# Another PSUM ring for the transposed probabilities of the second attention layer

## The chip, the core and the metric

The kernel runs on one core of a Trainium2 chip. The metric is the device time of one execution in microseconds (us), as the median of several runs. Lower is better. The core has five engines that run side by side, each with its own queue: TensorE (PE in the profile, with its weight loads as PEld), VectorE (DVE), ScalarE (ACT), GpSimd (POOL) and SyncE (SP), which issues the DMAs. TensorE writes its results to PSUM, which has eight banks here of 128 x 512 fp32 values each.

## What is computed

Two decoder layers on one sequence of 256 positions and 1024 features, in fp32. Layer 0 is causal attention with 16 heads (with 256 positions there is one block, so the block-sparse form comes down to that). Layer 1 is a sliding-window attention of width 128 with a learned sink per head; its 16 query heads share four key and value heads. After each attention comes a gated feed-forward part with a causal convolution of width 3. The attention of layer 1, which is the part that matters here, cut down:

```python
def swa_sink_attention(q, k, v, sinks):
    ...
    logits = jnp.einsum('bkgnqd,bknpd->bkgnqp', qb, kcat).astype(jnp.float32) * (HEAD_DIM ** -0.5)
    rel = (jnp.arange(WINDOW)[:, None] + WINDOW) - jnp.arange(2 * WINDOW)[None, :]
    band = (rel >= 0) & (rel < WINDOW)
    ...
    logits = jnp.where(mask, logits, NEG)
    ...
    m = jnp.maximum(jnp.max(logits, axis=-1, keepdims=True), sink)
    e = jnp.exp(logits - m)
    p = e / (jnp.sum(e, axis=-1, keepdims=True) + jnp.exp(sink - m))
    out = jnp.einsum('bkgnqp,bknpd->bkgnqd', p.astype(v.dtype), vcat)
```

With 256 positions there are two blocks of 128 queries. The first block sees its own 128 keys, the second sees all 256 (the window cuts a triangle out of each half).

## The kernel before, in words

**Precision.** Each large product is made of three fp32r products: both operands are split into a high and a low part, and high x high, high x low and low x high are added up in PSUM. The weights come from memory as raw fp32 units of 128 x 2048, and ACT writes their high part (`hi_part`, L181), DVE their low part (`lo_part`, L186 and L188). These conversions run all the time, for the weights that are needed a few units later.

**PSUM.** `bank(tag)` (L94) gives out the eight banks in three rings: four banks of tag `acc`, two of `t`, two of `u`. A bank comes free when the last reader of its tile is done. A new tile takes whichever bank of its tag is free.

**Attention.** `attention` (L405) works on four groups g = 0 to 3 of four heads each, and a group on two pairs of heads, j = 2g and 2g + 1. It serves both layers; `sink=True` is layer 1. For one group of layer 1 the steps are:

1. `scores` (L420). The scores of the first query block, called diagonal here, are six matmuls (L429 to L431) with full 128 rows into one bank, `sd`. That bank is of tag `acc` while the output projection has not begun to accumulate (groups 0 and 1), and of tag `t` afterwards (groups 2 and 3). The scores of the second block against all 256 keys are the half-row scores: twelve matmuls (L436) that each use only 64 of the 128 rows of TensorE, one head of a pair in the lower half and one in the upper, into two banks of tag `u`: `sb` for one head of each pair and `sa` for the other.
2. `softmax` (L441), for each pair: masked minima on DVE (L454, one instruction for a head's diagonal scores, one for its half-row scores), the exponentials on ACT (L465), on POOL the sum of the two halves of the second block's row (L460; `merge`, which the window allows), and the division by the row sum on DVE and ACT (L470 to L477).
3. `merged_T` (L485), for each pair: four transposes on TensorE (L490) into one PSUM bank, a copy by ACT (L499) and a masked product by DVE (L496) to SBUF. In layer 0 `probs_T` does this in another way.
4. `values` (L524): sixteen matmuls (L535) of the transposed probabilities with the values, into one bank of tag `t` (two banks for the last group), then a high part by ACT (L542) and a low part by DVE (L543).

In program order the scores of group g + 1 stand between the transposes of group g and its values.

**Filler.** Between these steps `fill` puts other TensorE work: the second half of the query projection (L342 to L344), and then the first three of the four units of the output projection (`Down`, L566; matmuls L584 to L587). Unit i of the output projection needs the values of group i. The query projection hands over its result by `to_feature` (L379): four transposes (L383) into a bank of tag `t`, then copies by ACT (L394) and DVE (L389). Its second half does this once for each query block, while groups 0 and 1 are in work. The scores of groups 2 and 3 read what it delivers: the diagonal ones need the first block's, the half-row ones the second block's. After the attention the last unit of the output projection follows (`finish`), then the feed-forward part, whose matmuls are L677 to L679.

**Order.** The order up to the first scores of layer 0 is that of the code. After that (`manual.close()`, L548) a scheduler orders each engine's queue when the program is built: it goes through the program with durations of its own, and an engine takes the instruction that stands first in program order among those whose inputs are there and for whose tile a bank of the tag is free. So a later instruction can be queued ahead of an earlier one that is not yet ready. (In the last group of layer 1 ACT alone keeps the program's order, L560.)

Of the kernel before, what the change touches and what calls it, by code (L numbers as in the profile page):

```python
# [61 lines left out]
def trunk(ctx: ExitStack, tc, x, xw, pos, cpk, fin, w, out):  # L62
# [9 lines left out]
    def nm(s):  # L72
        uid[0] += 1
        return f"{s}_{uid[0]}"
# [5 lines left out]
    def spaced(pool, n, dt, tag, name, bufs):  # L80
        return pool.tile([P, n + ROUND], dt, tag=tag, name=name, bufs=bufs)[:, SKIP:SKIP + n]
# [12 lines left out]
    def bank(tag):  # L94
        return ps.tile([P, 512], F32, tag=tag, name=nm(tag), bufs=4 if tag == "acc" else 2)
# [35 lines left out]
    def tick(ns):  # L131
        clock[0] += ns
        while put_off and not busy[0]:
            item = min(put_off, key=lambda t: t[0])
            if item[0] > clock[0]:
                return
            run_item(item)

    def chain(key, *steps, urgent=0):

        def run(k):
            if urgent:
                with tc.high_priority(offset=urgent):
                    steps[k][1]()
            else:
                steps[k][1]()
            if k + 1 < len(steps):
                put_off.append((clock[0] + steps[k + 1][0], key, lambda: run(k + 1)))
        put_off.append((clock[0] + steps[0][0], key, lambda: run(0)))
# [85 lines left out]
    for c in range(KC):  # L235
        t, at = (first[c // 2], KC * (c == 1) + c % 2 * CH) if c < 6 else (first[c - 3], 0)
# [26 lines left out]
    for b in range(NB):  # L263
        t = one.tile([P, NH, HD], F32, name=f"v{b}")
# [140 lines left out]
    def attention(qk, ready, filler, lead, rate, msk, vcol, sink):  # L405
# [78 lines left out]

        def merged_T(j, pr):  # L485

            tp = bank("u").rearrange("p (e k t) -> p e k t", e=2, k=2)
            for e in range(2):
                for k in range(2):
                    nc.tensor.transpose(tp[:, e, k], pr[e][:, 2 * k * P:(2 * k + 1) * P], ident)  # L490
            tick(440)
            pT = spaced(qd, 4 * S, F32, "q", nm("pT"), 15)[:, :6 * P].rearrange("p (e k t) -> p e k t", e=2, k=3)

            def part():
                shape = [P, 2, 2, P]
                nc.vector.tensor_tensor(out=pT[:, :, 1:], in0=tp[:, :, 1:].to_broadcast(shape),  # L496
                                        in1=near.unsqueeze(1).to_broadcast(shape), op=ALU.mult)

            chain(("pT", j), (200.0, lambda: nc.scalar.activation(pT[:, :, 0], tp[:, :, 0], AF.Copy)), (100.0, part))  # L499
            return [pT[:, e].rearrange("p k t -> p (k t)") for e in range(2)]  # L500

        def probs_T(j, pr):
            require("sm", j)
            if sink:
                return merged_T(j, pr)
            out_ = []
            for e in range(2):
                tp = bank("u")
                for i in range(3):
                    nc.tensor.transpose(tp[:, i * P:(i + 1) * P], pr[e][:, i * P:(i + 1) * P], ident)  # L510
                tick(330)
                pT = row3()

                def copy(e=e, tp=tp, pT=pT):
                    if e:
                        nc.scalar.activation(pT, tp[:, :3 * P], AF.Copy)
                    else:
                        nc.vector.tensor_copy(pT, tp[:, :3 * P])

                chain(("pT", j), (200.0, copy))  # L520
                out_.append(pT)
            return out_
# [666 lines left out]
```

## Time and profile before

| | |
|---|---|
| median of 3 runs | 549.57 us (549.19 to 550.01) |
| the profiled execution, its own time | 549.75 us |
| its span, first to last instruction | 548.0 us |
| granted TensorE clock | 0.998 |
| TensorE matmuls busy | 540.5 us (99%), 3742 matmuls |
| TensorE weight loads busy | 496.7 us (91%) |
| DVE, ACT, POOL busy | 420.4 us (77%), 372.9 us (68%), 125.3 us (23%) |
| transposes L490 (layer 1) | 32 matmuls, into tag `u` |
| half-row scores L436 of layer 1 | 48 matmuls, 316.9 to 348.7 us |
| values L535 of layer 1 | 64 matmuls, 327.2 to 358.6 us |

The time of an execution is a little longer than the span, since it holds what lies before the first and after the last instruction. In the rows of a timeline the first number is the start in us from the span's beginning, the second the duration of the row; a row can hold several instructions of a kind (x12). Matmuls overlap in the array, so a row's duration is longer than the distance to the next row, and the distance is what the engine spent. An arrow `u<-q,q` says that a tile of tag `u` was written from two tiles named `q`. A bracket like `[0.46 <-PE u L436]` says that the engine stood idle for 0.46 us before this row, and what ended the wait.

### The profile page before, as it was taken

To read this page: it belongs to the slowest core of one execution; us is meant where nothing else is said; L and a number is where in the kernel's file an instruction comes from. 1 tells how busy PE (TensorE), PEld (TensorE's weight loads), DVE (VectorE), ACT (ScalarE), POOL (GpSimd) and SP (SyncE) were. 2 spreads that over 40 slices of the span, in tenths; PEclk is the share of its full clock that TensorE was granted. 3 is DMA by queue.
4 is the path that set the end of the run, shared out by engine and by line. 5 is a ranking of instruction groups with operands and counts; after the bars stand their busy time and mean duration, and the time that the engine had idled before them with its cause. 6 is when DMAs were issued, how large, how long until landed. Compare 5 with 4: busy or idle time off the path is not lost.

```text
span 548.0 us, 9909 instructions
## 1 busy us (share of the span) xinstructions
PE 540.5 (99%) x3742; PEld 496.7 (91%) x3742; DVE 420.4 (77%) x872; ACT 372.9 (68%) x731; POOL 125.3 (23%) x158
## 2 busy tenths in 40 slices
PE   9999999999999999999999999999999999999995
PEld 8888888899999999988888887879999999998884
DVE  6798778689899888864467789798898888884514
ACT  6989777677677777744348688787667777673314
POOL 8322102016223233120001024102332332310003
PEclk9999999999999999999999999999999999999999
DMA  8984444342655565565553534242375555666301
GB/s 317 392 269 172 172 154 175 135 154 78 215 210 202 220 231 209 188 229 220 197 188 154 181 127 155 77 154 83 150 249 213 203 193 221 250 225 222 112 0 77
DMA packets 16464, 100.99 MB, mean 184 GB/s; under 512 B 1952, under 2 KB 2080, under 8 KB 5920
## 3 DMA queue, kind: packets, MB, share of 16 engines
q1 hardware_dynamic: 16128, 100.09, 50.5%
q8 instruction: 29, 0.48, 0.4%
q10 hardware_dynamic: 288, 0.26, 0.1%
q14 instruction: 19, 0.16, 0.1%
HBM read 99.30 MB, written 1.05 MB: 183 GB/s over the span
## 4 chain that ended last, share of the span: by engine, by line
PE 93%; ACT 3%; DVE 3%; issue 0%; DVEq 0%; ACTq 0%
PE acc L584 9%; PE acc L585 9%; PE acc L587 9%; PE u L677 7%; PE u L679 7%; PE u L678 7%; PE t L679 6%; PE t L678 6%; PE t L677 6%; PE acc L342 5%; PE acc L343 5%; PE acc L344 5%; PE acc L789 2%; PE acc L679 2%; PE acc L678 2%; PE acc L677 2%
## 5 line engine op out<-in xcount | busy, mean ns | idle before, releaser
L186 DVE TENSOR_TENSOR wl<-wr,wh 128x1024 fp32r<-128x1024 f32 (+1 forms) x190 | 207.9, 1114 | 52.2 <-ACT wh L181 51.7
L181 ACT ACTIVATE wh<-wr 128x1024 fp32r<-128x1024 f32 (+1 forms) x190 | 176.5, 957 | 52.6 <-PE acc L587 42.8
L723 POOL TENSOR_TENSOR m<-m,m 128x256 f32<-128x256 f32 x44 | 70.4, 1601 | 166.5 <-DVE m L718 91.9
L584 PE MATMUL acc<-wh,q 128*128 128x512 f32 x238 | 92.4, 388 | 0.1
L585 PE MATMUL acc<-wl,q 128*128 128x512 f32 x238 | 90.8, 381 | 0.0
L677 PE MATMUL u<-q,wh 128*128 128x256 f32 x320 | 88.4, 277 | 0.0
L678 PE MATMUL u<-q,wh 128*128 128x256 f32 x320 | 88.2, 276 | 0.0
L679 PE MATMUL u<-q,wl 128*128 128x256 f32 x320 | 88.1, 276 | 0.0
L679 PE MATMUL t<-q,wl 128*128 128x256 f32 x288 | 79.3, 275 | 0.0
L677 PE MATMUL t<-q,wh 128*128 128x256 f32 x288 | 79.3, 275 | 0.0
L678 PE MATMUL t<-q,wh 128*128 128x256 f32 x288 | 79.3, 275 | 0.0
L587 PE MATMUL acc<-wh,q 128*128 128x512 f32 x238 | 75.4, 382 | 0.0
L678 PEld LDWEIGHTS u<-q,wh 128*128 128x128 f32 x320 | 61.5, 192 | 0.0
L679 PEld LDWEIGHTS u<-q,wl 128*128 128x128 f32 x320 | 61.5, 192 | 0.0
L677 PEld LDWEIGHTS u<-q,wh 128*128 128x128 f32 x320 | 61.3, 192 | 0.2 <-DVE q L305 0.2
L677 PEld LDWEIGHTS t<-q,wh 128*128 128x128 f32 x288 | 55.4, 192 | 0.0
L678 PEld LDWEIGHTS t<-q,wh 128*128 128x128 f32 x288 | 55.4, 192 | 0.0
L679 PEld LDWEIGHTS t<-q,wl 128*128 128x128 f32 x288 | 55.4, 192 | 0.0
L584 PEld LDWEIGHTS acc<-wh,q 128*128 128x128 f32 x238 | 45.1, 190 | 6.9 <-ACT q L542 0.9
L587 PEld LDWEIGHTS acc<-wh,q 128*128 128x128 f32 x238 | 44.9, 189 | 6.5 <-DVE q L543 0.3
L585 PEld LDWEIGHTS acc<-wl,q 128*128 128x128 f32 x238 | 45.2, 190 | 5.8 <-issue 0.3
L342 PE MATMUL acc<-wh,q 128*128 128x512 f32 x128 | 49.9, 390 | 0.0
(177 smaller groups left out, 1008.5 us busy)
## 6 DMA issues: line engine op xcount, KB each, us to landing
wr<-in_w SPq DMA_DIRECT2D x82, 1024.0 KB, 4.8
wr<-in_w SPq DMA_DIRECT2D x16, 512.0 KB, 6.4
first<-in_xw SPq DMA_DIRECT2D x7, 384.0 KB, 6.4
xr<-in_x SPq DMA_DIRECT2D x2, 512.0 KB, 8.0
fin_t<-in_fin SPq DMA_DIRECT2D x1, 512.0 KB, 5.5
out<-ot SPq DMA_DIRECT2D x1, 512.0 KB, 2.6
first<-in_xw SPq DMA_DIRECT2D x1, 388.0 KB, 3.5
out<-m ACTq DMA_DIRECT2D x1, 256.0 KB, 2.1
```

The costliest lines, as they stand in the source:

```text
L181: nc.scalar.activation(wq[i][0][:, c], raws[i][:, c], AF.Copy, **({} if g is None else {"scale": g}))
L186: nc.vector.tensor_tensor(out=lo, in0=raw, in1=hi, op=ALU.subtract)
L342: nc.tensor.matmul(o, xh[:, blk(b)], wh, start=(c == 0), stop=False)
L343: nc.tensor.matmul(o, xh[:, blk(b)], wl, start=False, stop=False)
L344: nc.tensor.matmul(o, xl[:, blk(b)], wh, start=False, stop=(c == KC - 1))
L584: nc.tensor.matmul(o, ph[:, blk(b)], turns(hi[:, s_]), start=first, stop=False)
L585: nc.tensor.matmul(o, ph[:, blk(b)], turns(lo[:, s_]), start=False, stop=False)
L587: nc.tensor.matmul(o, pl[:, blk(b)], turns(hi[:, s_]), start=False, stop=end)
L677: nc.tensor.matmul(o, hi[:, s_], xh, start=(c == 0), stop=False)
L678: nc.tensor.matmul(o, hi[:, s_], xl, start=False, stop=False)
L679: nc.tensor.matmul(o, lo[:, s_], xh, start=False, stop=(c == KC - 1))
L723: nc.gpsimd.tensor_tensor(out=h, in0=gs, in1=t[1], op=ALU.mult)
```

## The change

`merged_T` takes its bank from ring `t` and no longer from ring `u`. It is called only in layer 1, once for each of the eight pairs. Nothing else differs: the instructions, their sizes and the program order are the same.

```diff
         def merged_T(j, pr):
 
-            tp = bank("u").rearrange("p (e k t) -> p e k t", e=2, k=2)
+            tp = bank("t").rearrange("p (e k t) -> p e k t", e=2, k=2)
             for e in range(2):
                 for k in range(2):
                     nc.tensor.transpose(tp[:, e, k], pr[e][:, 2 * k * P:(2 * k + 1) * P], ident)
```

After it, ring `u` serves in this stage only `sa` and `sb` (two tiles for each group), and ring `t` serves the transposed probabilities (two tiles for each group), the values (one, in the last group two), the diagonal scores of groups 2 and 3, and the two `to_feature` tiles of the second half of the query projection.

## The prediction

> **What bounds the kernel now.** I read the page first.
>
> ```profile
> span 548.0 us, 9909 instructions
> ...
> PE 540.5 (99%) x3742; PEld 496.7 (91%) x3742; DVE 420.4 (77%) x872; ACT 372.9 (68%) x731; POOL 125.3 (23%) x158
> ...
> PE 93%; ACT 3%; DVE 3%; issue 0%; DVEq 0%; ACTq 0%
> ```
>
> TensorE is busy nearly everywhere, and 93% of the chain that ended last is TensorE work. So what TensorE no longer spends, or no longer waits for, in the attention of layer 1 comes off the end, since the feed-forward part behind it is its own back-to-back work. The table by stretches, from the values of one group to those of the next (groups 0 to 3), shows how full the others are there:
>
> ```profile
> 327.20:338.60 11.40, 11.19 (x74) 8.45 (x73) 10.88 (x40) 9.29 (x28) 4.76 (x8) 1.00 0.38 134
> 338.60:348.70 10.10, 10.10 (x66) 8.05 (x65) 8.66 (x29) 8.32 (x28) 2.13 (x4) 1.00 0.23 73
> 348.70:357.20 8.50, 8.50 (x54) 6.71 (x53) 6.47 (x23) 6.13 (x21) 1.95 (x4) 1.00 0.25 107
> ```
>
> After the length come PE, PEld, DVE, ACT and POOL. In the first stretch DVE has 10.88 of 11.40 us, so there the chain of softmax steps can't get shorter by an earlier start alone. Then I read DVE's timeline:
>
> ```profile
> 334.60 1.23 DVE L186 TENSOR_TENSOR wl<-wr,wh 128x1024 fp32r<-128x1024 f32 x1 [0.34 <-ACT wh L181]
> 335.75 0.68 DVE L496 TENSOR_TENSOR pT<-u,v 128x512 f32<-128x512 f32 x1
> 336.35 0.68 DVE L389 TENSOR_TENSOR q<-t,q 128x512 fp32r<-128x512 f32 x1
> 336.94 0.68 DVE L496 TENSOR_TENSOR pT<-u,v 128x512 f32<-128x512 f32 x1
> 337.54 0.34 DVE L454 CUSTOM_DVE_ANT_0 m<-t,mask,nsink 128x128 f32<-128x128 f32 x1
> ...
> 340.48 0.16 DVE L470 RECIPROCAL hst<-hst 128x2 f32<-128x2 f32 x1
> ...
> 344.63 0.69 DVE L496 TENSOR_TENSOR pT<-u,v 128x512 f32<-128x512 f32 x1 [0.65 <-ACT pT L499]
> 345.58 1.23 DVE L186 TENSOR_TENSOR wl<-wr,wh 128x1024 fp32r<-128x1024 f32 x1 [0.25 <-ACT wh L181]
> 346.72 0.69 DVE L496 TENSOR_TENSOR pT<-u,v 128x512 f32<-128x512 f32 x1
> 347.32 0.34 DVE L454 CUSTOM_DVE_ANT_0 m<-t,mask,nsink 128x128 f32<-128x128 f32 x1
> ...
> 348.80 0.48 DVE L454 CUSTOM_DVE_ANT_0 m<-u,mask,nsink 128x256 f32<-128x256 f32 x1 [0.46 <-PE u L436]
> ...
> 356.40 0.69 DVE L496 TENSOR_TENSOR pT<-u,v 128x512 f32<-128x512 f32 x1 [0.93 <-ACT pT L499]
> ```
>
> The minima of a group (L454) begin in the moment in which the masked product (L496) of the group before is done: at 337.54 and 347.32. From one to the next is 9.78 us, and from 347.32 to the end of the last L496 (356.40 + 0.69) 9.77. The attention is thus paced by a chain of four links of about 10 us, minima to masked product, and TensorE fills the time with projections. Both are balanced: the fillers end about when the chain does. A gain has to come off both.
>
> **The change part by part.** *Removed: the transposes no longer hold the banks of the half-row scores.* TensorE's timeline:
>
> ```profile
> 316.94 0.98 PE L436 MATMUL u<-q,q 64*128 64x256 f32 x12
> 317.86 0.48 PE L343 MATMUL acc<-wl,q 128*128 128x512 f32 x1
> ...
> 325.91 1.33 PE L436 MATMUL u<-q,q 64*128 64x256 f32 x12
> 327.17 1.52 PE L535 MATMUL t<-pT,v 128*64 128x256 f32 x16
> ...
> 337.19 1.46 PE L436 MATMUL u<-q,q 64*128 64x256 f32 x12
> 338.58 1.52 PE L535 MATMUL t<-pT,v 128*64 128x256 f32 x16
> 340.03 0.48 PE L587 MATMUL acc<-wh,q 128*128 128x512 f32 x1
> ...
> 346.05 0.97 PE L436 MATMUL u<-q,q 64*128 64x256 f32 x6
> 346.95 0.48 PE L584 MATMUL acc<-wh,q 128*128 128x512 f32 x1
> ...
> 347.79 0.97 PE L436 MATMUL u<-q,q 64*128 64x256 f32 x6
> 348.69 1.52 PE L535 MATMUL t<-pT,v 128*64 128x256 f32 x16
> ...
> 357.17 1.52 PE L535 MATMUL t<-pT,v 128*64 128x256 f32 x16
> ```
>
> In group 0, with both banks free, twelve half-row matmuls take 0.92 us (316.94 to 317.86): the two halves of the array work side by side. In the other groups one bank comes later than the other, because it holds transposes not yet copied. Then one half runs alone: 1.26 us (325.91 to 327.17), 1.39 (337.19 to 338.58), and in group 3 six of the one bank in 0.90 and six of the other in 0.90, as long as twelve together. The scheduler had queued them apart. After the change `sa` and `sb` need only the minima of the group before, which are done some 5 us earlier. Freed TensorE time: 0.34 + 0.47 + 0.88 = 1.69 us. Group 3 also saves an interruption for each of its two sixes, which I leave out.
>
> On the chain this shows only where the minima waited for L436: in group 3, 0.46 us (row 348.80). With its scores early, DVE can also use the 0.25 us of idle time before L186 at 345.58 for a minimum. Together 0.71 us. In groups 1 and 2 the chain gains nothing: DVE has no hole there.
>
> *Added: tenants of ring t.* The four transposes of a pair, L499 and L496 are the same instructions, and no DMA moves. What is new is who waits for whom, from these rows of TensorE, ACT and DVE:
>
> ```profile
> 323.70 0.60 PE L383 MATMUL t<-ident,m 128*128 128x128 f32 x4
> ...
> 334.42 0.49 PE L490 MATMUL u<-ident,m 128*128 128x128 f32 x3
> 334.74 0.60 PE L383 MATMUL t<-ident,m 128*128 128x128 f32 x4
> ...
> 335.27 0.36 PE L429 MATMUL t<-kd,q 128*128 128x256 f32 x1
> ...
> 340.35 0.30 PE L429 MATMUL t<-kd,q 128*128 128x256 f32 x1
> ...
> 345.30 0.60 PE L490 MATMUL u<-ident,m 128*128 128x128 f32 x4
> ```
>
> ```profile
> 335.38 0.61 ACT L394 ACTIVATE q<-t 128x512 fp32r<-128x512 f32 x1 [0.25 <-PE t L383]
> 335.87 0.38 ACT L499 ACTIVATE pT<-u 128x256 f32<-128x256 f32 x1
> ...
> 345.94 0.38 ACT L499 ACTIVATE pT<-u 128x256 f32<-128x256 f32 x1 [0.39 <-PE u L490]
> ```
>
> ```profile
> 324.89 1.32 DVE L496 TENSOR_TENSOR pT<-u,v 128x512 f32<-128x512 f32 x2
> ```
>
> - First `to_feature` (323.70): both banks now hold pairs 0 and 1, so it waits for the first of the two L496, to about 325.5. Behind it in program order stand the scores of group 1, which are ready and go ahead, and nobody reads its result before the scores of group 2. I cost it at nothing; without that cover it is 1.8 us.
> - Second `to_feature` (334.74): it waits for pair 2's L496, to 336.35. From there as in the rows: L394 0.64 us later (336.99), L389 when that is done (337.6), L436 0.84 after L389's start (337.19 less 336.35), at 338.44 and no longer at 337.19. In exchange pair 3's L496 moves up, into L389's place at 336.35. The diagonal scores of group 2 (335.27) then take pair 3's bank at 336.95. Behind them on TensorE wait the half-row scores and the values of group 1, and these hold up unit 1 of the output projection. DVE's eight minima took 2.94 us (337.54 to 340.48); begun at about 337.3, with L389's 0.60 between them, they end at 340.84, 0.36 late. Part of that is hidden: in this link pair 5's L496 (346.72) stands behind an L186, while its L499 was done at 346.32. So 0.40 of lateness costs the chain nothing. Bounds: nothing, or 0.8, if the late end of L436 (338.44 + 0.92 against 338.58) is passed on whole. I take 0.1, near the row with the cover.
> - Group 2: at 340.35 the diagonal scores of group 3 take a bank of t ahead of the transposes. If they do so again, pair 5 needs pair 4's bank, free at the end of L496, 345.2 to 345.3. Its transposes ran at 345.30 anyway: nothing. With an L186 in front of that L496, as at 334.60, it is 1.1 us.
> - Values take the bank of a pair whose copy they wait for in any case: nothing.
>
> The TensorE side must agree. In group 1 its fillers are used up early, since it waits for the chain: its values end at 338.44 + 0.92 + 1.45 = 340.8, and no longer at 340.03, so 0.8 is lost there. The last matmul of unit 0, which followed them (0.32 us, 340.03 to 340.35), is then done already, and group 3's scores give back 0.88 more. That is 0.4 us less, and more with the two interruptions that I left out. The chain says 0.71 - 0.1 = 0.6. I take the chain's 0.6.
>
> Against the profiled execution's own 549.75 us the sum is 549.15. It was 0.18 above the median of 549.57, so in the median's terms 549.0.
>
> A rule speaks against the change: the Trainium skill, in Perfetto Trace Analysis, section Optimizing Tensor Performance, says that independent matmul groups should rotate through different PSUM banks, so that copying one out overlaps the next one's matmuls. By the rule, five tiles a group on two banks lose overlap; the rows give it a price of nothing to 1.1 us per handover. Taken whole it is the third rival below.
>
> **The rivals.** *TensorE alone sets the end.* If the scheduler, with the scores free to move, fills the chain's holes (0.65 and 0.25 before 344.63 and 345.58, 0.93 before 356.40), the whole 1.69 us come off: 547.9. For it: DVE has 1.4 of 10.1 us and 2.0 of 8.5 us free in the last two stretches. Against it: 10.88 of 11.40 in the first, and TensorE's new waits there.
>
> *Nothing comes through.* The last link keeps its 9.77 us, since ACT's steps, not L454, end its waits (0.93 at 356.40): 549.6.
>
> *Ring t serialises group 1, the end on the other side.* The diagonal scores or `to_feature` take the second bank before pair 3's transposes do. Pair 3 then starts at 336.35 and not at 334.42, and `to_feature` waits for pair 3's L496 as well: another handover of transposes 0.60, L499 0.38 and L496 0.60 (rows 345.30, 345.94, 346.72 to 347.32). L436 comes at about 340.0, 2.8 us late. The minima, half of whose 2.94 us needs L436, end at about 341.9, 1.4 late. TensorE, out of fillers, loses up to 2.8 less the 0.47. At 1.9 between the two, less the 0.6, the result is 550.9. It decides if the second tenant's first matmul is queued before 334.42. Against it: pair 3 is ahead in program order. For it: TensorE is ahead of time by then and takes what is ready.
>
> **How the numbers follow.** 0.2%, about what a measurement of this kernel can tell from no change, is 1.1 us: 548.5 and 550.7 are the bounds. The forecast (549.0) has 0.40, of it 0.05 beyond the faster bound and 0.01 beyond the slower. TensorE alone (547.9) has 0.28, of it 0.02 within. Nothing (549.6) has 0.10. Ring t (550.9) has 0.22, of it 0.02 within. So faster 0.31, same 0.48, slower 0.21. The range goes from 547.3 (1.69 and the 0.6 of other waits) to 551.2 (1.6 lost). Within the likeliest case it is 548.3 to 549.8.
>
> **What would show it.** Right: L436 is four rows of x12 of about 0.92 us. L383 begins after pair 2's L496 (about 336.4), the half-row scores of group 2 at about 338.4. The row at 348.80 has lost its wait, and the last values begin at about 356.6. Wrong: L436 still split, or the last values after 357.2. The forecast falls if in group 1 `to_feature` or the diagonal scores are queued before pair 3's transposes, or if the values of group 1 begin before 338.6, which would speak for the first rival.

## The result, and the profile after

The changed kernel takes 552.53 us (median of 6 runs, 552.30 to 553.07) where before takes 549.61 beside it: a ratio of 1.0055, 95% interval 1.0046 to 1.0065, or 2.9 us slower. Forecast were 549.0 and a range up to 551.2. Its profiled execution took 552.66 us with a span of 550.9 at the same granted clock, 0.998. The page of the changed kernel:

```profile
span 550.9 us, 9916 instructions
...
PE 540.0 (98%) x3742; PEld 494.9 (90%) x3742; DVE 421.4 (76%) x872; ACT 373.0 (68%) x731; POOL 121.6 (22%) x158
...
PE 91%; DVE 4%; ACT 3%; issue 1%; DVEq 0%; ACTq 0%
```

TensorE is busy for 0.5 us less than before (540.0 for 540.5), and the span is 2.9 longer. So TensorE waits 3.4 us more. The table by stretches of the changed kernel, from the values of one group to those of the next, shows where:

```profile
326.29:341.03 14.74, 12.39 (x78) 8.97 (x76) 13.52 (x42) 12.14 (x33) 3.83 (x8) 1.00 0.42 143
341.03:350.73 9.70, 8.68 (x63) 6.87 (x61) 7.02 (x25) 5.66 (x22) 1.84 (x4) 1.00 0.30 110
350.73:360.09 9.36, 9.30 (x56) 7.16 (x55) 7.03 (x27) 6.91 (x25) 2.02 (x4) 1.00 0.00 1
```

The first stretch has become 3.3 us longer (14.74, before 11.40), and in it TensorE stands idle for 2.35 us, before for 0.21. The second has 1.02 us of idle TensorE. Where this is on TensorE's timeline of the changed kernel:

```profile
324.35 0.86 PE L436 MATMUL u<-q,q 64*128 64x256 f32 x10
325.39 0.66 PE L383 MATMUL t<-ident,m 128*128 128x128 f32 x4 [0.17 <-DVE pT L496]
325.98 0.38 PE L436 MATMUL u<-q,q 64*128 64x256 f32 x2
326.29 1.52 PE L535 MATMUL t<-pT,v 128*64 128x256 f32 x16
...
337.11 0.66 PE L383 MATMUL t<-ident,m 128*128 128x128 f32 x4
337.71 0.38 PE L429 MATMUL t<-kd,q 128*128 128x256 f32 x1
...
340.12 0.98 PE L436 MATMUL u<-q,q 64*128 64x256 f32 x12 [1.48 <-DVE q L389]
341.03 1.52 PE L535 MATMUL t<-pT,v 128*64 128x256 f32 x16
...
343.56 0.49 PE L436 MATMUL u<-q,q 64*128 64x256 f32 x2 [1.00 <-DVE hst L454]
...
348.62 0.60 PE L490 MATMUL t<-ident,m 128*128 128x128 f32 x4
...
349.82 0.98 PE L436 MATMUL u<-q,q 64*128 64x256 f32 x10
350.73 1.52 PE L535 MATMUL t<-pT,v 128*64 128x256 f32 x16
```

What the change was to do has happened: from group 2 on L436 runs side by side (0.91 from 340.12 to 341.03, before 1.39; ten in 0.91 from 349.82, the other two being the row at 343.56; before twelve in 1.80), and the values of group 0 begin 0.9 earlier (326.29, before 327.17). But the second `to_feature` tile (L383) starts at 337.11 and not at 334.74, and L436 of group 2 at 340.12 and not at 337.19. DVE's timeline of the changed kernel says why:

```profile
335.24 1.22 DVE L186 TENSOR_TENSOR wl<-wr,wh 128x1024 fp32r<-128x1024 f32 x1
336.38 1.28 DVE L496 TENSOR_TENSOR pT<-t,v 128x512 f32<-128x512 f32 x2
338.24 1.23 DVE L186 TENSOR_TENSOR wl<-wr,wh 128x1024 fp32r<-128x1024 f32 x1 [0.59 <-ACT wh L181]
339.38 0.69 DVE L389 TENSOR_TENSOR q<-t,q 128x512 fp32r<-128x512 f32 x1
339.99 0.34 DVE L454 CUSTOM_DVE_ANT_0 m<-t,mask,nsink 128x128 f32<-128x128 f32 x1
...
341.07 1.22 DVE L186 TENSOR_TENSOR wl<-wr,wh 128x1024 fp32r<-128x1024 f32 x1
342.20 0.48 DVE L454 CUSTOM_DVE_ANT_0 m<-u,mask,nsink 128x256 f32<-128x256 f32 x1
...
349.68 0.69 DVE L496 TENSOR_TENSOR pT<-t,v 128x512 f32<-128x512 f32 x1 [1.91 <-ACT pT L499]
...
359.31 0.69 DVE L496 TENSOR_TENSOR pT<-t,v 128x512 f32<-128x512 f32 x1 [1.29 <-ACT pT L499]
```

And ACT's timeline of the changed kernel:

```profile
337.15 1.06 ACT L181 ACTIVATE wh<-wr 128x1024 fp32r<-128x1024 f32 x1 [0.70 <-PE acc L587]
338.12 0.58 ACT L394 ACTIVATE q<-t 128x512 fp32r<-128x512 f32 x1
```

Read them as one story. Pair 2's masked product (L496, 336.38) holds the bank for which the tile waits, and it stands behind a weight conversion (L186, 335.24). When the tile is transposed at last, ACT has just begun another conversion (337.15), and L394 comes behind that. DVE, which has nothing of the softmax to do, waits 0.59 us for ACT and then takes the low part of the same conversion (338.24), so L389 comes behind that too. The conversions at 338.24 and 341.07 are those of weight unit 59, which before ran at 342.36 and 345.58, when the minima were over. Only after L389 come the minima of group 2, with the second half of the conversion in their midst. They begin at 339.99 (before 337.54), the last ends at 343.9 (before 340.5). Nothing gives that back: the minima of group 3 begin 2.96 us later than before (350.28, before 347.32), and the last link takes 9.81 us (to 360.09; before 9.85, from 347.32 to 357.17).

### The profile page after: what moved, and what is told of

Read it like the earlier page. It is cut to its first block, busy times and chain, and to the rows that moved or that the text cites. A ratio compares the mean times of both kernels' runs of the same rounds, so it can differ in the third digit from the quotient of the medians.

```text
span 550.9 us, 9916 instructions
## 1 busy us (share of the span) xinstructions
PE 540.0 (98%) x3742; PEld 494.9 (90%) x3742; DVE 421.4 (76%) x872; ACT 373.0 (68%) x731; POOL 121.6 (22%) x158
## 3 DMA queue, kind: packets, MB, share of 16 engines
HBM read 99.30 MB, written 1.05 MB: 182 GB/s over the span
## 4 chain that ended last, share of the span: by engine, by line
PE 91%; DVE 4%; ACT 3%; issue 1%; DVEq 0%; ACTq 0%
PE acc L584 8%; PE acc L587 8%; PE acc L585 8%; PE u L677 7%; PE u L678 6%; PE u L679 6%; PE t L677 6%; PE t L678 6%; PE t L679 6%; PE acc L342 5%; PE acc L344 5%; PE acc L343 5%; PE acc L789 2%; PE acc L679 2%; PE acc L678 2%; PE acc L677 2%
## 5 line engine op out<-in xcount | busy, mean ns | idle before, releaser
L186 DVE TENSOR_TENSOR wl<-wr,wh 128x1024 fp32r<-128x1024 f32 (+1 forms) x190 | 207.1, 1109 | 49.2 <-ACT wh L181 49.0
L181 ACT ACTIVATE wh<-wr 128x1024 fp32r<-128x1024 f32 (+1 forms) x190 | 176.3, 955 | 48.9 <-PE acc L587 42.3
L723 POOL TENSOR_TENSOR m<-m,m 128x256 f32<-128x256 f32 x44 | 69.0, 1569 | 168.5 <-DVE m L718 91.9
```

Of the source, the lines that this page charges most:

```text
L181: nc.scalar.activation(wq[i][0][:, c], raws[i][:, c], AF.Copy, **({} if g is None else {"scale": g}))
L186: nc.vector.tensor_tensor(out=lo, in0=raw, in1=hi, op=ALU.subtract)
L723: nc.gpsimd.tensor_tensor(out=h, in0=gs, in1=t[1], op=ALU.mult)
```

## Experiments

Each ran in five rounds beside the kernel before. Times are medians; the ratio is to before on the same chip, with its 95% interval. In the later columns times are us from the first L436 of layer 1 (which itself starts at 315.7 to 317.1), in the profiled execution: the start of the second `to_feature` tile (L383), of L436 of group 2, of the last minimum (L454) of group 2, and of the last values.

| kernel | us | ratio | L383 | L436 | last min. | values |
|---|---|---|---|---|---|---|
| before | 549.57 | | 17.8 | 20.3 | 23.1 | 40.2 |
| changed | 552.53 | 1.0055 [1.0046, 1.0065] | 20.4 | 23.4 | 26.7 | 43.4 |
| e7 changed, tile in `u` | 549.74 | 1.0005 [0.9996, 1.0014] | 18.8 | 21.3 | 23.8 | 40.6 |
| e2 changed, group 1 in `u` | 549.91 | 1.0008 [0.9999, 1.0017] | 18.8 | 21.2 | 23.9 | 40.6 |
| e3 before, group 1 in `t` | 551.85 | 1.0048 [1.0035, 1.0061] | 19.6 | 22.5 | 25.8 | 42.6 |
| e8 changed, short conv. | 549.50 | 1.0002 [0.9993, 1.0011] | 18.2 | 20.6 | 23.4 | 40.2 |
| e14 changed, short 58 | 550.37 | 1.0018 [1.0009, 1.0027] | 18.6 | 21.5 | 25.0 | 41.2 |
| e13 changed, short 59 | 551.65 | 1.0042 [1.0029, 1.0054] | 20.4 | 23.1 | 25.8 | 42.3 |
| e9 before, short conv. | 550.11 | 1.0012 [1.0004, 1.0021] | 17.8 | 20.4 | 23.1 | 40.9 |
| e12 before, tile in `u` | 549.07 | 0.9994 [0.9985, 1.0003] | 19.6 | 22.0 | 24.6 | 39.8 |
| e15 changed, diagonals of 2 in `u` | 551.13 | 1.0032 [1.0020, 1.0045] | 19.5 | 22.0 | 25.3 | 41.7 |
| e5 first pairs in `t` | 551.30 | 1.0031 [1.0019, 1.0044] | 18.6 | 21.3 | 23.9 | 41.8 |
| e6 second pairs in `t` | 550.63 | 1.0021 [1.0012, 1.0030] | 18.9 | 21.9 | 25.5 | 41.3 |
| e17 before, 4 L436 a group | 549.49 | 1.0003 [0.9994, 1.0012] | 18.7 | 20.3 | 24.3 | 41.1 |
| e18 changed, 4 L436 a group | 550.33 | 1.0025 [1.0016, 1.0034] | 19.9 | 21.6 | 26.3 | 42.0 |
| e10 changed, tile in `u`, short conv. | 548.03 | 0.9975 [0.9966, 0.9985] | 17.4 | 20.3 | 22.8 | 38.9 |
| e19 before, tile in `u`, short conv. | 549.41 | 1.0000 [0.9991, 1.0009] | 18.6 | 21.2 | 23.4 | 40.2 |
| e20 as e10, both tiles in `u` | 549.07 | 0.9993 [0.9984, 1.0001] | 18.4 | 21.3 | 23.7 | 40.0 |

The theory after the result: the loss is made in group 1 by the second `to_feature` tile, which in ring `t` waits for pair 2's masked product, and by the conversions that come in front of its two copies. The rivals: the loss is elsewhere (other groups, or TensorE's own time); or the conversions alone make it. A letter in a quoted expectation means what that text says of it.

### The place: e7, e2, e3

**e7.** The changed kernel with only the second tile of `to_feature` back out of ring `t`; `ring` is handed through `rotate` to `to_feature`.

```diff
-        pt = bank("t")
+        pt = bank(ring)
...
-                   turn=2500.0 if a else 1000.0)
+                   turn=2500.0 if a else 1000.0, ring="u" if a and b else "t")
```

> As changed, but the to_feature tile of the second query block of the query projection's second half (the one at 337.1 us in the changed kernel) takes ring u. Theory A (this tile's wait for pair 2's bank is the loss): its transposes come back to about 334.8 us, the half-row scores of group 2 to about 337.2 (340.1 in the changed kernel), and the time falls by 2.4 to 3.4 us from 552.5, to 549.1 to 550.1. Theory B (the conversions L181 and L186 that stand in front of the copies and the minima are the loss, whichever ring the tile has): at most 1 us less, 551.5 or more. Theory C (the transposes in t lose in every group, by values and diagonal scores): 551 or more.

**e2** (changed, only group 1's transposes back in ring `u`) and **e3** (before, only group 1's moved to ring `t`):

```diff
-            tp = bank("t").rearrange(...)
+            tp = bank("u" if j // 2 == 1 else "t").rearrange(...)
```
```diff
-            tp = bank("u").rearrange(...)
+            tp = bank("t" if j // 2 == 1 else "u").rearrange(...)
```

> As changed, but the two pairs of group 1 keep ring u as before. Theory A: the second to_feature tile finds a bank of t, the loss is gone; group 2's half-row scores again run one half after the other (0.5 us more of TensorE), group 3's are cheaper: 549.0 to 549.9. Theory B: 551.5 or more. Theory C: a third of the loss gone, about 551.5.

> As before, but the two pairs of group 1 take ring t. Theory A: the whole loss or more, 552 to 553.5, since nothing is gained in groups 2 and 3. Theory B: between 549.6 and 552.5, by how the conversions fall. Theory C: a third of the loss, about 550.5.

The loss goes with the tile alone (549.74) and with group 1 alone (549.91), and group 1 alone brings 2.4 of its 2.9 us (551.85). So it is made in group 1, through that tile. The other three groups' moved transposes neither cost nor gain: with e7 and e2 the last values stand at 40.6, before at 40.2. That was a surprise for the gain, and comes back below. An edit moves the order of the queues elsewhere too: of the 2.8 us by which e7's last values come sooner than the changed kernel's, 0.4 arise only behind the first minimum of group 3.

### Conversions: e8, e14, e13, e9

The conversions of weight units 57 to 60 in four pieces of 512 columns and no longer two of 1024 (one piece on DVE 0.68 us in place of 1.22); in e14 only those of unit 58, in e13 of unit 59, in e9 all four in the kernel before.

```diff
-        n = 4 if i <= 5 or ... or U_KV <= i <= U_OB else 2
+        n = 4 if i <= 5 or ... or U_KV <= i <= U_OB or 57 <= i <= 60 else 2
```

> As changed, but the conversions of the four weight units of this stretch (numbers 57 to 60) come in pieces of 128x512 and no longer of 128x1024 (L181 about 0.6 us instead of 1.05, L186 0.65 instead of 1.2; some 16 instructions more). Theory B: what stands in front of the second to_feature tile's copies and of group 2's minima halves: L181 at 337.15, L186 at 338.24 and at 341.07, together 2.7 us, become about 1.4, and the time falls by 1 to 1.5 us, to 551.0 to 551.5. Theory A: the wait for pair 2's bank stays, the pieces that fill the holes come one after another all the same: 0 to 0.7 us less, 551.8 to 552.6.

> As changed, with short conversions for unit 58 alone, the ones that run before the tile and stand in front of pair 2's masked product (L181 at 333.51, L186 at 333.51 and 335.24). Theory A: pair 2's bank comes free about 1.2 us earlier, so the tile starts at about 335.9 (337.1 as changed) and the time falls by 1.5 to 3 us, to 549.5 to 551. Theory B: the conversions of unit 59 still stand in front of its copies, 0 to 0.8 less, 551.7 to 552.6.

> As changed, with short conversions for unit 59 alone, the ones that run behind the late tile (L181 at 337.15 and 338.59, L186 at 338.24 and 341.07). The tile stays late, at about 337. Theory B: the copies and minima wait half as long for them, half-row scores of group 2 at about 339.3 (340.1 as changed), and 0.8 to 1.5 us less, 551.0 to 551.7. Theory A alone: no more than 0.4 less, 552.1 to 552.6.

> The kernel before with the short conversions of units 57 to 60 alone (the control for the changed kernel with them, 549.5). Theory A+B (the late second to_feature tile and the whole conversions behind it make the loss together, and short ones only take away what the ring change had added): 549.2 to 549.8, the same as before. Theory D (short conversions are worth about 3 us in any kernel, and the ring change still costs its own): 546.6 to 548.

Short pieces alone take the whole loss away (549.50), with the tile still in ring `t`. In the kernel before they gain nothing and rather cost something (550.11), so it is the change's loss that they cure and not one that was there. Unit 58, which stands in front of pair 2's L496, carries most of it: with it short the loss is 1.0 us against before beside it, no longer 2.9. With unit 59 short it is still 2.3, and since the interval of e13 overlaps that of the changed kernel, this smaller part isn't told apart from nothing. DVE's timeline of e14:

```profile
333.99 0.67 DVE L186 TENSOR_TENSOR wl<-wr,wh 128x512 fp32r<-128x512 f32 x1
334.78 0.68 DVE L496 TENSOR_TENSOR pT<-t,v 128x512 f32<-128x512 f32 x1
335.57 1.28 DVE L186 TENSOR_TENSOR wl<-wr,wh 128x512 fp32r<-128x512 f32 x2
```

Pair 2's L496 now starts at 334.78, between two pieces, and no longer at 336.38. The tile follows at 18.6 and not 20.4.

### A late tile by itself: e12, e15

**e12.** The kernel before, with the second tile in ring `u`. The transposes are there, so the tile waits for pair 2 exactly as in the changed kernel; the edit is e7's.

> The kernel before, where only the second to_feature tile goes to ring u, where the transposes of pairs 2 and 3 hold both banks; the transposes stay in u, nothing is added to t. The tile waits for pair 2's bank as it does in the changed kernel. Theory A+B: the loss appears without the change, its transposes at 336.4 or later, group 2's half-row scores at 339 to 340.5, and 551 to 553. Theory C (it is the crowd in t): 549.5 to 550.

The tile is late (19.6, 1.8 later than before), and L436 as well (22.0), but nothing is lost: 549.07. That falsifies the plain form of the theory. DVE's timeline of e12 shows the difference:

```profile
333.62 0.33 DVE L454 CUSTOM_DVE_ANT_0 m<-t,mask,nsink 128x128 f32<-128x128 f32 x1
...
335.51 1.28 DVE L496 TENSOR_TENSOR pT<-u,v 128x512 f32<-128x512 f32 x2
336.71 0.34 DVE L454 CUSTOM_DVE_ANT_0 m<-t,mask,nsink 128x128 f32<-128x128 f32 x1
...
337.76 0.69 DVE L389 TENSOR_TENSOR q<-u,q 128x512 fp32r<-128x512 f32 x1 [0.16 <-ACT q L394]
```

Ring `t` is free there, so the diagonal scores of group 2 began at 328.92 already, and DVE does the last three of their four minima while the tile is on its way. In the changed kernel these scores take the next bank of `t` behind the tile (337.71). In e7 the scores are nearly as late (336.87) with the tile sooner (335.24), and there is no loss either. So of four cases (neither late: before; scores late: e7; tile late: e12; both: changed) only the last one loses. But e12 differs in one thing more. There the values of group 1 come ahead of the half-row scores of group 2 and not behind them, so TensorE too has work while the tile is on its way, and unit 1 of the output projection isn't held up as in the changed kernel. TensorE's timeline of e12:

```profile
336.25 0.65 PE L383 MATMUL u<-ident,m 128*128 128x128 f32 x4
336.84 1.52 PE L535 MATMUL t<-pT,v 128*64 128x256 f32 x16
...
338.71 0.97 PE L436 MATMUL u<-q,q 64*128 64x256 f32 x12
```

Which of the two spares e12 the loss, the early minima or the early values, no run separates.

**e15** was to test this the other way round: changed, with the diagonal scores of group 2 in ring `u`.

```diff
-            sd, sa, sb = bank("t" if o_down[0].acc else "acc"), bank("u"), bank("u")
+            sd, sa, sb = bank("u" if sink and g == 2 else "t" if o_down[0].acc else "acc"), bank("u"), bank("u")
```

> The changed kernel, but the diagonal scores of group 2 take a bank of ring u (the half-row scores of that group then wait in one bank for the diagonal minima). The second to_feature tile keeps its bank of ring t and stands behind pair 2's transposes there, as in the changed kernel. Theory A (the late tile by itself costs the time: L436 of group 2 can't start before it): 552 to 553 us, as changed, last values at about 360. Theory B (the late tile costs the time only because the diagonal scores stand behind it in the same ring, so that DVE has nothing of the softmax to do while the tile is late, and takes weight conversions): L383 late (336 to 337) and L436 of group 2 late (338.5 to 340), but the diagonal minima run while the tile is on its way, and the time is 549.0 to 550.3 us, last values before 358. Rival C (ring u's banks, shared now by three tiles in group 2, cost as much as was won): about 551, with L436 of group 2 split into two sixes.

It doesn't decide. The scores ran early (13.9), but three of the four diagonal minima were still queued behind L389, and L436 of group 2 came in two sixes, 1.5 us apart (338.69 and 340.17), as its rival C had it. 551.13 is 1.4 below the changed kernel, and how much of it either effect has stays open.

### Half of the change: e5, e6

```diff
-            tp = bank("u").rearrange(...)
+            tp = bank("u" if j % 2 else "t").rearrange(...)
```

(e5, against before; e6 has `"t"` and `"u"` the other way round.)

> Half of the change: in each group the first pair's transposes go to ring t, the second pair's stay in ring u. No tile of to_feature stands behind transposes that are still to be copied, so by A and by B the loss is gone: 549.0 to 550.2 us, L383 of the second tile before 335.5. If the chain of softmax steps sets the end, the moved half brings nothing either (within 0.5 us of before); if half of TensorE's freed time came through, 548.5.

> The other half: the second pair's transposes go to ring t, the first pair's stay in ring u. By A and by B the loss is gone here too, since the tile finds the bank of group 0's values free: 549.0 to 550.2 us, L383 of the second tile before 335.5. In groups 1 and 2 L436 runs side by side (about 0.92 us) if pair 2's and pair 4's banks in ring u are copied in time. If TensorE's freed time came through, 548.5; by the chain within 0.5 us of before.

Both missed: 551.30 and 550.63. The tile is 0.8 and 1.1 us late, though it waits for no masked product. In both, pair 2's L496 starts 0.9 us later than before (19.7 us after the first L436, before 18.8), as it does in the changed kernel and in e7. e7 loses nothing by it, so their loss is something else. The columns place e5's: up to the last minimum of group 2 it stands as e7 does (23.9 and 23.8), and its last values come 1.2 us later. By the rows of ACT and TensorE, 0.9 of this is a wait of the last pair. In e5 its probabilities are ready at 355.80 (end of L475), but its transposes start at 357.02, behind matmuls of the output projection; in e7 the two are 354.89 and 355.18. In e6 that wait is 1.22 us as in e5, in the changed kernel 1.01, before 0.66. So TensorE's order in the last group moves the end as well, with no part of the tile in it. No run tests this by itself.

### Is it TensorE's time: e17, e18

Four L436 for a group in place of twelve: the products high x low and low x high of the half-row scores are left out in layer 1.

```diff
-                for k, (q_, k_) in enumerate(((ql, kh_), (qh, kl_), (qh, kh_))):
+                for k, (q_, k_) in enumerate(((ql, kh_), (qh, kl_), (qh, kh_))[2 if sink else 0:]):
...
-                                         start=(k == 0), stop=(k == 2))
+                                         start=(k == 0), stop=sink or k == 2)
```

> The kernel before, with only one of the three products in the half-row scores of layer 1 (high x high; the two with a low part are left out, so these scores are less exact): four L436 for a group and no longer twelve. The rows of before give 0.92 + 1.26 + 1.39 + 1.80 us of TensorE for the twelves, two thirds of which is 3.6 us, about twice what the change could free. If TensorE's time sets the end, the time falls by about 3.6 us, to 546. If the chain from minima to masked product sets it, freed TensorE time is worth little: 548.7 to 549.8 us, and the links stay near 9.8 us.

> The changed kernel with the same two products left out (high x low and low x high of the half-row scores in layer 1). If the loss is TensorE's own time in its waits, the freed time pays it back: about 549. If it is the chain (the late tile, and the diagonal minima behind it), the time stays above 551, with L389 of the second tile again at 338 or later.

In the kernel before, the products left out bring nothing: 549.49, ratio 1.0003. The TensorE time freed is less than the 3.6 us expected: the page of e17 has TensorE busy for 538.5 us, before for 540.5, and by the distances between rows L436 takes 3.0 us in place of 5.4, since in groups 2 and 3 it runs two and two. Some 2.0 to 2.4 us are still more than the 1.69 us that the change was to free. The table by stretches of e17, from values to values:

```profile
327.06:339.30 12.24, 10.61 (x63) 7.50 (x62) 11.76 (x39) 9.27 (x29) 4.11 (x8) 1.00 0.36 117
339.30:349.12 9.82, 9.60 (x58) 7.29 (x57) 8.88 (x31) 8.10 (x28) 2.38 (x4) 1.00 0.31 110
349.12:357.60 8.48, 8.20 (x51) 6.38 (x50) 6.47 (x23) 6.09 (x21) 1.95 (x4) 1.00 0.19 78
```

TensorE now has 1.63, 0.22 and 0.28 us idle where it had 0.21 and none, and the stretches are together no shorter (30.5, before 30.0). TensorE's time doesn't set the end. The order moved here too (pair 3's L496 stands at 21.7 us after the first L436, before at 20.0), so the run shows that freed TensorE time alone isn't worth anything, not what a chain left untouched would take. In the changed kernel the same edit saves about 2 us (550.33; 551 and more was expected by the chain, 549 by TensorE). L389 came at 336.88 there, not at 338 or later, so the order had moved as well, and this run can't be put down to either.

### Both remedies: e10, e19, e20

**e10** is the changed kernel with e7's and e8's edits together, **e19** the kernel before with both. **e20** is e10 with the first `to_feature` tile in ring `u` as well (`ring="u" if a else "t"`).

> The changed kernel with both remedies: the second to_feature tile in ring u, and the conversions of weight units 57 to 60 in four pieces each. If the two remedies take away one and the same loss, and the chain sets the rest, 549.2 to 550.2 us, as with each alone. If a second loss is left in each of them that the other removes, below 549.0, and the change would then bring its gain after all.

> The kernel before with both remedies (the second to_feature tile in ring u, conversions of units 57 to 60 in four pieces) but without the change: the transposes stay in ring u. It is the control of the run that reached 548.03. If the change is what brings the 1.3 us there, by the half-row scores that run side by side, this one stays at 549.0 to 550.3. If the remedies bring it by themselves, about 548.0, and the change is worth nothing in any company.

> The changed kernel with the short conversions and with both to_feature tiles of the second half of the query projection in ring u. The first tile waited for a masked product in ring t as well (325.39 instead of 323.70). If that wait costs nothing, as predicted, 547.7 to 548.5, as with the second tile alone; if it costs something in group 1, 547.3 or less; if the first tile stands in the way of group 1's half-row scores in ring u, 548.6 or more.

e10 beats both kernels: 548.03, ratio 0.9975 [0.9966, 0.9985]. The remedies without the change don't (549.41, ratio 1.0000), so beside e19 it is the change that brings 1.4 us. Against e12, the fastest kernel without the change (ratio 0.9994), it is 1.0. What the change does thus hangs on its company: +2.9 us alone; 549.07 to 549.74 with the tile in `u` (e12, e7) and 550.11 to 549.50 with short conversions (e9, e8), neither told apart from nothing, since the intervals overlap; -1.4 with both. TensorE's timeline of e10:

```profile
324.19 0.39 PE L436 MATMUL u<-q,q 64*128 64x256 f32 x2
324.51 0.66 PE L383 MATMUL t<-ident,m 128*128 128x128 f32 x4
325.10 0.86 PE L436 MATMUL u<-q,q 64*128 64x256 f32 x10
325.88 1.52 PE L535 MATMUL t<-pT,v 128*64 128x256 f32 x16
...
336.85 0.97 PE L436 MATMUL u<-q,q 64*128 64x256 f32 x12
...
345.07 0.97 PE L436 MATMUL u<-q,q 64*128 64x256 f32 x12
```

L436 runs side by side, ten and two in group 1 and all twelve in groups 2 and 3. From the first L436, the last minimum of group 1 starts at 11.91 us (e19: 12.38), that of group 2 at 22.76 (23.42), that of group 3 at 31.61 (32.91). So 0.47 us are won up to the first of them, 0.19 up to the second, 0.64 up to the third and 0.04 behind. DVE's timeline of e19 has the two places where a minimum waits for a half-row score; in e10 none does:

```profile
327.14 0.48 DVE L454 CUSTOM_DVE_ANT_0 m<-u,mask,nsink 128x256 f32<-128x256 f32 x1 [0.60 <-PE u L436]
...
348.36 0.48 DVE L454 CUSTOM_DVE_ANT_0 m<-u,mask,nsink 128x256 f32<-128x256 f32 x1 [0.62 <-PE u L436]
```

The wait in group 3 is the one that the forecast had counted on; before has it too (0.46 at 348.80). The one in group 1 is e19's own: there L436 of group 1 comes in two sixes, before it does not.

In e20 the first tile in ring `u` stands in the way of the scores of group 1, which come in sixes again (TensorE's timeline of e20), and the gain is gone:

```profile
325.05 0.97 PE L436 MATMUL u<-q,q 64*128 64x256 f32 x6
...
327.81 0.97 PE L436 MATMUL u<-q,q 64*128 64x256 f32 x6
```

## Why the prediction was wrong, point by point

**The chain as the bound: right.** In e17 at least 2.0 us of freed TensorE time bring nothing, with the reserve stated there. That speaks against the first rival (547.9, TensorE alone), which had 0.28.

**L436 side by side: right as a mechanism, absent from the end.** In the changed kernel L436 is no longer split by halves, but in groups 1 and 3 two of the twelve ran apart from the ten, so the rows give 0.08 + 0.48 + 0.47 = 1.03 us of freed TensorE time and not 1.69. The minima of group 3 wait for it no more. Yet the 0.71 us are not in the last link, which takes 9.81 us for 9.85. That is what the second rival (nothing comes through) had said: ACT's step ends the wait of the last L496, and this wait has grown from 0.93 us to 1.29 (359.31). The last pair's transposes, queued behind the output projection, now start 1.01 us after its probabilities are ready, before 0.66. In e10 the change is worth 1.4 us beside e19, of which 0.64 are made between the last minima of groups 2 and 3, where the forecast had put 0.71.

**First `to_feature`: right.** It began at 325.39, forecast 325.5. Nor does taking it out of the ring win anything (e20), but there it stood in the way of the scores, so its price in ring `t` by itself stays open.

**Second `to_feature`: the step that failed.** It was costed at 0.1, with bounds from nothing to 0.8. The working followed a fixed order of DVE's and ACT's instructions, only later, and filled no hole. Forecast and measured: L383 at 336.35 and 337.11, L394 at 336.99 and 338.12, L389 at 337.6 and 339.38, L436 at 338.44 and 340.12. Most of the 1.68 us between the last two come from three conversions. The one in front of pair 2's L496 started at 335.24, before at 334.60, and so L496 0.63 later; the tile came 0.76 later than forecast, with two matmuls of the output projection just ahead of it. One on ACT in front of L394 added 0.37, one on DVE in front of L389 0.65; and L436 followed L389 0.10 sooner than in the rows of before. The Trainium skill, in Perfetto Trace Analysis, section Tensor Engine Instruction, says that ACT, DVE and GpSimd are strictly first in, first out; the trace agrees, L394's result being there at 338.70 and L389 starting when the conversion in front of it lets go, at 339.38. The minima were forecast to begin ahead of L389 and to end at 340.84, 0.36 late, with 0.40 of cover behind. Their scores came out of ring `t` 0.76 late as well, directly behind the tile, and on DVE the minima stood behind L389, with the second half of the conversion in their midst. They ended at 343.9, 3.4 us later than before. A cover of 0.40 does not reach that far. By the first minimum of group 2 the step cost 2.45 us (339.99, before 337.54), where the sum had 0.1.

**Group 2: costed at nothing, 0.5 measured.** From the first minimum of group 2 to that of group 3 it is 10.29 us, before 9.78. No L186 stood in front, as its bound had it. Pair 5's transposes (348.62) stood behind ten matmuls of the output projection that ran from 346.38 on, late themselves because the values of group 1 were, and ACT waited for them:

```profile
ACT pT L499 <- PE t L490: 4.4, 3, 2.2
...
PE u L436 <- DVE q L389: 1.5, 1, 1.5
...
PE u L436 <- DVE hst L454: 1.0, 1, 1.0
```

In this list of waits of the changed kernel (305 to 372 us; in all, times, longest) the 2.2 is that wait of pair 5.

**The third rival** had the side and the place, and its price of 1.3 over no change was less than half of the 2.9. Its mechanism did not occur: pair 3's transposes were queued ahead of the tile and of the diagonal scores. The rule of the Trainium skill that was weighed there (Perfetto Trace Analysis, Optimizing Tensor Performance: groups should rotate through different PSUM banks) points the right way for the changed kernel. By the runs it is one tile whose sharing costs, and only beside whole conversions: with short ones it shares without a loss (549.50), and with that tile elsewhere as well the time falls (548.03), though the other tiles of ring `t` still share two banks.

**Range.** Its upper end, 551.2, was built from 1.6 us lost. The profile of before held what was missing: whole conversions of 1.22 us on DVE and 1.05 on ACT, one of each within 2 us of the tile's copies (334.60 and 333.52). That they move into a hole that a wait opens is shown by unit 59's (338.24, before 342.36).

## What to carry to other kernels

When a scheduler orders the queues, a wait that a change adds is not a shift of the rows behind it: price it together with the longest off-path instruction that can slip into the hole, on every engine that the waiting tile passes through. Here two tiles of one ring cost nothing when either came late, and 2.9 us when both did, the second being work for which the engine could have used the wait; so look at what stands next in the same ring. And when a sound idea comes out slower, undo its side effects one at a time and then together: here each remedy alone led back to zero, and only both showed what the idea was worth, 1.0 to 1.4 us by the kernel without the change that it is held against.
